# Cutting the first store of an RMSNorm-GELU kernel in three and joining the last two

## Chip, cores and metric

The kernel runs on one core of a Trainium2 chip. The metric is device time in microseconds (us), the median of several executions. "The packet records" below are the single DMA packets that the trace of the profiled execution holds, each with queue, start, duration and size.

## The reference

```python
rms = np.sqrt(np.mean(x ** 2, axis=-1, keepdims=True) + eps)
out = gamma * x / rms
return 0.5 * out * (1 + np.tanh(np.sqrt(2 / np.pi) * (out + 0.044715 * out ** 3)))
```

`x` is 8 x 1024 x 2048 in float32: 67.1 MB are read and 67.1 MB are written, with little arithmetic on each element.

## The kernel before

The 8192 rows are cut into 16 groups of 512 rows, four rows (32 KB) on each of 128 partitions, 4 MB a group. Six slots of SBUF hold groups in flight; slots lie two by two in one tile, so that two groups can share a transfer. SyncE issues the loads, ScalarE (ACT) the stores. ScalarE and VectorE (DVE) square and sum, VectorE multiplies by gamma, ScalarE applies the GELU in place, and the slot is stored.

```python
LOAD_PAIR = 1
STORE_PAIR = 6
NARROW = 128
    ...
def gelu(g):
    for r in range(R):                  # R = 4 rows
        nc.scalar.activation(out=slot[g % SLOTS][:, r, :], in_=slot[g % SLOTS][:, r, :],
                             func=ACT.Gelu_apprx_tanh, scale=rstd[:, g, r : r + 1])

def store(g):
    if g:
        if g // 2 != STORE_PAIR:
            nc.scalar.dma_start(out=part(o2, g), in_=slot[g % SLOTS])
        elif g % 2:
            nc.scalar.dma_start(out=pair_part(o2, g // 2), in_=pair[g // 2 % (SLOTS // 2)])
        return
    src = pair[0].rearrange("p r d -> p (r d)")
    dst = part(o2, 0).rearrange("p r d -> p (r d)")
    for a, z in ((0, NARROW), (NARROW, R * D)):
        nc.scalar.dma_start(out=dst[:, a:z], in_=src[:, a:z])
    ...
for g in range(G + 1):                  # G = 16
    ...                                 # squares, 1/rms and gamma of group g
    if g:
        gelu(g - 1)
        store(g - 1)
        if g - 1 + SLOTS < G:
            load(g - 1 + SLOTS)
```

Group 0 leaves in two stores, the first with 512 bytes of each partition. Groups 12 and 13 leave in one store. The load of group 6 needs slot 0, so it waits for all of group 0's stores.

## Time and profile before

| | before |
|---|---|
| time, median of the first 3 executions | 317.21 us (316.85 to 317.45) |
| span of the profiled execution | 315.1 us |
| busiest compute engine | ScalarE, 66% |
| DMA queues, share of 16 engines' time | loads 49.7%, stores 49.3% |
| bytes moved | 134.24 MB |

The two queues' shares add up to 99.0% of the time of the core's 16 DMA engines; the prediction works out what follows.

### The profile page before, as it was taken

What the parts mean: (1) busy time and instruction counts of PE and PEld (TensorE: products, weight loads), DVE (VectorE), ACT (ScalarE), POOL (GpSimd) and SP (SyncE); (2) the same over time, 40 slices, a digit from 0 to 9 for tenths busy, and PEclk for the clock granted to TensorE, in tenths of its full rate; (3) what the DMA queues carried; (4) which work ended last, traced back from release to release, by engine and by line L of the source; (5) the groups of instructions that cost most, each with busy time, mean ns of one, the idle gap of its engine ahead of it and who ended that gap; (6) DMA issues with size and microseconds to landing.
All of it is one profiled execution on the core that took longest, in us unless ns stands there. A gap on an engine that the chain in (4) does not pass through costs nothing.

```text
span 315.1 us, 457 instructions
## 1 busy us (share of the span) xinstructions
PE 7.2 (2%) x8; PEld 2.5 (1%) x8; DVE 198.5 (63%) x129; ACT 206.9 (66%) x150; POOL 16.4 (5%) x21
## 2 busy tenths in 40 slices
PE   0900000000000000000000000000000000000000
PEld 0300000000000000000000000000000000000000
DVE  0089887988989884639684393668727638781000
ACT  1327869999999749397590965929369295797000
POOL 0010101011010101010010100101001010010000
DMA  8999989999999999999999999999999999999896
GB/s 334 404 462 408 526 339 396 458 402 462 403 463 403 459 408 458 412 453 424 441 424 441 424 441 424 441 428 437 437 428 437 428 437 428 474 399 474 387 445 291
DMA packets 4498, 134.24 MB, mean 426 GB/s; under 512 B 512, under 2 KB 656, under 8 KB 656
## 3 DMA queue, kind: packets, MB, share of 16 engines
q1 hardware_dynamic: 2160, 67.11, 49.7%
q10 hardware_dynamic: 2336, 67.12, 49.3%
q14 instruction: 2, 0.02, 0.0%
HBM read 67.12 MB, written 67.11 MB: 426 GB/s over the span
## 4 chain that ended last, share of the span: by engine, by line
another core or an unknown queue 36%; DMA 36%; ACT 18%; issue 1%; SPq 1%; ACTq 0%
DMA pair<-in_x_dram 21%; DMA out_dram<-pair 15%; ACT pair L133 12%; ACT junk L87 6%; SPq L83 1%; ACTq L143 0%
## 5 line engine op out<-in xcount | busy, mean ns | idle before, releaser
L124 DVE TENSOR_TENSOR pair<-pair,gamma_ps 128x8192 f32<-128x8192 f32 (+1 forms) x19 | 139.2, 7334 | 0.0
L87 ACT ACTIVATE junk<-pair 128x2048 f32<-128x2048 f32 x42 | 79.0, 1881 | 78.7 <-DMA pair<-in_x_dram 76.2
L133 ACT ACTIVATE pair<-pair,rstd 128x2048 f32<-128x2048 f32 x64 | 122.6, 1987 | 2.3 <-DVE pair L124 1.9
L97 DVE SCALAR_TENSOR_TENSOR spare<-pair 128x2048 f32<-128x2048 f32 x22 | 50.4, 2291 | 39.3 <-DMA pair<-in_x_dram 24.6
L110 POOL TENSOR_TENSOR y<-ms,power 128x4 f32<-128x4 f32 x16 | 16.1, 1007 | 260.8 <-DVE ms L105 260.8
L105 DVE TENSOR_SCALAR ms<-ssq 128x4 f32<-128x4 f32 x16 | 2.7, 170 | 26.2 <-ACT junk L87 25.4
L113 DVE TENSOR_TENSOR z<-ms,y 128x4 f32<-128x4 f32 x16 | 2.6, 163 | 19.0 <-POOL y L110 19.0
L87 ACT ACTIVATION_READ_ACCUMULATOR junk<-pair 128x1 f32 x42 | 7.8, 186 | 0.0
L171 PE MATMUL gamma_ps<-spare,ones 1*128 1x512 f32 x8 | 7.2, 1072 | 8.3 <-DMA spare<-in_gamma_dram 8.3
L117 DVE SCALAR_TENSOR_TENSOR rstd<-z,y 128x4 f32<-128x4 f32 x16 | 2.6, 162 | 0.6
L114 DVE SCALAR_TENSOR_TENSOR z<-z,y 128x4 f32<-128x4 f32 x16 | 2.6, 162 | 0.6
L171 PEld LDWEIGHTS gamma_ps<-spare,ones 1*128 1x128 f32 x8 | 2.5, 326 | 11.4 <-issue 11.4
L169 ACT ACT_TABLE_LOAD x1 | 1.3, 1283 | 1.4 <-PEq L211 1.4
L97 DVE DVE_READ_ACCUMULATOR spare<-pair 128x1 f32 x22 | 1.8, 83 | 0.0
L167 DVE MEMSET warm<- 1x1 f32 x1 | 0.1, 59 | 0.8 <-PEq L211 0.8
L169 ACT ACTIVATE warm<-warm 1x1 f32<-1x1 f32 x1 | 0.2, 202 | 0.0
L168 DVE MEMSET ones<- 1x128 f32 x1 | 0.2, 165 | 0.0
L166 POOL MEMSET power<- 128x4 f32 x1 | 0.1, 101 | 0.3 <-POOLq L211 0.3
L211 POOL MEMSET const-float32-0.0<- 128x1 f32 x1 | 0.1, 98 | 0.2 <-issue 0.2
L211 POOL MEMSET const-bfloat16-1.0<- 128x1 bf16 x1 | 0.1, 102 | 0.0
L211 POOL MEMSET const-uint8-127<- 128x1 uint8 x1 | 0.1, 102 | 0.0
L211 POOL MEMSET const-float32-1.0<- 128x1 f32 x1 | 0.1, 98 | 0.0
## 6 DMA issues: line engine op xcount, KB each, us to landing
pair<-in_x_dram SPq DMA_DIRECT2D x14, 4096.0 KB, 25.5
out_dram<-pair ACTq DMA_DIRECT2D x13, 4096.0 KB, 52.4
out_dram<-pair ACTq DMA_DIRECT2D x1, 4032.0 KB, 31.3
out_dram<-pair ACTq DMA_DIRECT2D x1, 64.0 KB, 17.6
spare<-in_gamma_dram ACTq DMA_DIRECT2D x1, 8.0 KB, 7.4
pair<-in_x_dram SPq DMA_DIRECT2D x1, 40.5
out_dram<-pair ACTq DMA_DIRECT2D x1, 30.9
```

Source lines behind the costliest of these rows:

```text
L83: nc.sync.dma_start(out=slot[g % SLOTS], in_=part(x2, g))
L87: nc.scalar.activation(out=junk, in_=slot[g % SLOTS][:, q, :], func=ACT.Square, accum_out=ssq[:, g, q : q + 1],)
L97: nc.vector.scalar_tensor_tensor(out=spare[:, :, 0:GW], in0=row, scalar=1.0, in1=row, op0=ALU.bypass, op1=ALU.mult, accum_out=ssq[:, g, q ...
L105: v.tensor_scalar(out=ms, in0=ssq[:, g, :], scalar1=1.0 / D, scalar2=eps_f, op0=ALU.mult, op1=ALU.add,)
L110: nc.gpsimd.tensor_tensor(out=y_, in0=m_, in1=power, op=ALU.pow)
L113: v.tensor_tensor(out=z_, in0=m_, in1=y_, op=ALU.mult)
L114: v.scalar_tensor_tensor(out=z_, in0=z_, scalar=-0.5, in1=y_, op0=ALU.mult, op1=ALU.mult)
L117: v.scalar_tensor_tensor(out=rstd[:, g, :], in0=z_, scalar=1.5, in1=y_, op0=ALU.add, op1=ALU.mult,)
L124: nc.vector.tensor_tensor(out=rows, in0=rows, in1=gamma_ps.unsqueeze(1).to_broadcast([P, n, D]), op=ALU.mult,)
L133: nc.scalar.activation(out=slot[g % SLOTS][:, r, :], in_=slot[g % SLOTS][:, r, :], func=ACT.Gelu_apprx_tanh, scale=rstd[:, g, r : r + 1],)
L169: nc.scalar.activation(out=warm, in_=warm, func=ACT.Gelu_apprx_tanh)
L171: nc.tensor.matmul(out=gamma_ps[:, k : k + 512], lhsT=ones, rhs=gamma_row[:, k // GW : (k + 512) // GW, 0:GW], start=True, stop=True,)
```

## The change

The intent: group 0's two first rows can leave before the last two are done; the last two groups save a transfer. The number of transfers stays at 32. (`part` follows because the rows of a joined pair lie together: groups 14 and 15 are now also loaded by the rows of a pair, with the same packet size.)

```diff
-STORE_PAIR = 6
+STORE_PAIRS = (6, 7)
@@ part
-        if g // 2 in (LOAD_PAIR, STORE_PAIR):
+        if g // 2 in (LOAD_PAIR, *STORE_PAIRS):
@@ store
-            if g // 2 != STORE_PAIR:
+            if g // 2 not in STORE_PAIRS:
@@
-        for a, z in ((0, NARROW), (NARROW, R * D)):
+        for a, z in ((0, NARROW), (NARROW, R * D // 2), (R * D // 2, R * D)):
```

## The prediction

> **What bounds the kernel now.** I read first the page: the span, the busy shares, the DMA rows of the slices, and the packet counts.
>
> ```profile
> span 315.1 us, 457 instructions
> PE 7.2 (2%) x8; PEld 2.5 (1%) x8; DVE 198.5 (63%) x129; ACT 206.9 (66%) x150; POOL 16.4 (5%) x21
> DMA  8999989999999999999999999999999999999896
> DMA packets 4498, 134.24 MB, mean 426 GB/s; under 512 B 512, under 2 KB 656, under 8 KB 656
> q1 hardware_dynamic: 2160, 67.11, 49.7%
> q10 hardware_dynamic: 2336, 67.12, 49.3%
> ```
>
> No compute engine is above 66%, while the 16 DMA engines are at nine tenths or more nearly everywhere. Loads (q1) and stores (q10) take 99.0% of the DMA engines' time together. Next, the busy-by-stretch view, in the middle of the run (its last two columns are the DMA share and GB/s; a short stretch misleads there, because a packet is counted whole where it starts), then the DMA view of the stretch from the landing of the last load to the landing of the second-last stores:
>
> ```profile
> 90.00:250.00 160.00, 0.00 (x0) 0.00 (x0) 108.35 (x66) 108.55 (x78) 8.44 (x9) 1.00 1.00 433
> ```
>
> ```profile
> DMA packets 240, 11.01 MB, mean 433 GB/s; under 512 B 32, under 2 KB 32, under 8 KB 32
> q10 hardware_dynamic: 240, 11.01, 100.1%
> ```
>
> So 433 GB/s is what the engines give, with both queues working and with the store queue alone. The chain of waits then shows what holds the loop together:
>
> ```profile
> 127.99 0.33 SPq L83
> 128.32 18.86 another core or an unknown queue
> ...
> 147.25 0.33 SPq L83
> 147.58 18.99 another core or an unknown queue
> ```
>
> Loads are issued 19.26 us apart. One load and one store are 8.39 MB, and 8.39 MB / 433 GB/s is 19.37 us: the period is the transfer time, with nothing left over. The waits of the SyncE queue name the releaser, a store that frees a slot:
>
> ```profile
> SPq L83 <- DMA out_dram<-pair: 236.9, 11, 47.3
> ```
>
> The whole: the first packet starts at 1.74 us; 134.24 MB / 433 GB/s is 310.0 us; the last packet ends at 313.9, the last store lands at 314.3, and the closing barrier is 0.8. 313.9 - 1.7 - 310.0 leaves 2.2 us. The trace's packet records show where most of it is: the first packets of the run take 1.5 to 2.2 us instead of 1.21 (about 0.75 us averaged over 16 engines), and from 46 to 49.4 us a round of load packets takes about 1.75 us instead of 1.21 (about 0.65). The latter comes just after the 512-byte store of group 0. The measured 317.21 is the span plus some 2 us outside it.
>
> [...] on one engine I read, from 50.6 us on, a load packet (1213 ns), a store packet (1194), a load packet and so on; and earlier a 512-byte packet (27 ns) after each load packet. [...] The trace shows receipts (a packet's end to the landing, about 0.3 us at the end), but no engine idles for one, as the next transfer is queued. [...]
>
> **The change, part by part.** *Count.* Group 0 goes from two stores to three, groups 14 and 15 from two to one. Each of those transfers has 128 data packets and 16 semaphore packets (14 x 144 + 144 = 2160 on q1), so both queues keep their counts: 2160 and 2336, with the same bytes.
>
> *Packet time.* The records have 27 ns for 512 B, 1194 for 32256 B, 1213 for 32768 B and 2418 for 65536 B: a straight line of 36.8 ps per byte plus 8 ns a packet. An engine has 8 packets of each store. Group 0 now: 8 x (27 + 1194) = 9.77 us per engine. After: 15872 B is 592 ns, 16384 B is 611, so 8 x (27 + 592 + 611) = 9.84. Added: 0.07 us. Groups 14 and 15 now: 16 x 1213 = 19.41; after: 8 x 2418 = 19.34. Removed: 0.07 us. Sum: 0.00.
>
> *Start of group 0's stores.* The narrow store is issued at 32.79 us, as row 0 ends, and the remainder at 38.47, as row 3 ends. The new second store waits for row 1 only, so goes out near 34.7. It gains nothing there: the eight 512-byte packets of an engine each wait for a load packet of up to 2.4 us, so the ring reaches the next store only at 49.4 us on that engine either way. The extra issue is 0.34 us on ACT, which then idles 3.7 us before 42.16.
>
> *Order on the engine.* Round robin is per packet, not per byte. Eight packets of 32256 B against load packets of 32768 B shared the engine half and half, from 49.4 to 67.4. With packets of half the size the loads get two thirds: laying the packets of that engine out by hand, the second store ends at 61.4, the last load packet of group 5 at 67.4 (before 73.4), then the third store runs alone to 71.1. So group 5 should land near 69 instead of 75.3, and group 0's store near 73 instead of 69.7; the load of group 6 goes out some 3.5 us later than its 69.8. No byte is lost: the store queue holds the stores of groups 1 and 2 (issued at 55.8 and 67.9), which fill the load's gap.
>
> *Tail.* Group 14's store was issued at 281.29 and group 15's at 289.38. Merged, it goes out at 289.0 (one issue of 0.34 us less before group 15's rows). The store of groups 12 and 13 lands at 294.95, its first engines done at 293.9. From issue to first packet takes about 1 us at the run's start (0.74 to 1.74), so the merged store is ready at about 290.4, 3.5 us ahead of need. Then 8.39 MB / 433 = 19.37 us gives 314.3, the old landing.
>
> Sum: +0.07 - 0.07, start, dip and barrier unchanged: **317.2 us**, the same.
>
> **The rivals.** *The tail starves.* If the ring had been empty by 281.29, merging would cost the 8.1 us to 289.38: 325 us. Against it is the view of 269.6 to 295 above: 100.1% busy on earlier stores alone. It needs group 15 to finish 3.5 us later than it does. *The later load tears a hole.* If the 3.5 us delay of group 6's load went round the ring of slots to the end: near 321 us. Against it: stores land 48.6 us after issue at the median, so more than two stores lie queued, and steady transfers make good such a shift. *The dip moves.* The slow round of load packets at 46 to 49.4 us sits where the 512-byte packets end. If the size of the next store's packets matters, it can vanish or come twice: 316.6 or 317.9. I take it as unchanged. *A shared semaphore stalls ACT.* Transfers take eight semaphores in turn, and each waits for the earlier user; one more transfer early shifts the turn by one. ACT's chain shows 0.14 us at 73.99 and 0.52 at 284.95 around such waits. A stall of a few us on ACT in the middle hides behind queued stores; at the end it must exceed the 3.5 us. *The intent:* with smaller second packets the loads come earlier, but compute isn't the bound, so an earlier group 5 buys nothing.
>
> **Range and chances.** Everything that moves is a matter of order in queues that stay full; what can alter the sum is the dip (0.65 us either way) and the spread of runs (316.85 to 317.45). So 8 times in 10 from 316.4 to 318.1. Two per cent is 6.3 us: faster by that is impossible with 310.0 us of transfer in it, short of fewer bytes; slower needs the tail to starve nearly in full. Chances: faster 0.005, same 0.98, slower 0.015.
>
> **What would show it.** Right: 4498 packets and the same counts per queue; 433 GB/s in the middle and the tail; issue of the merged store near 289.0, last landing near 314.3; the load of group 6 issued near 73 us; the second store issued near 34.7. Wrong: a zero in the DMA row of any slice but the ends, an issue of the last store after 293, or loads spaced by more than 19.4 us. A difference of over 1 us with a DMA row full of nines would mean that packets take longer by size or order than the line above says.

What the part on order rests on, that packets of the two queues take turns whatever their size, is in the packet records of the kernel before, chained into engines by their times: on one engine, from 36.5 to 46.4 us, each of eight 512-byte packets (27 ns) goes between two load packets (2418 or 1213 ns; once, at 41.41 us, a 4-byte load packet of 9 ns), and from 49.4 to 67.4 us load packets (1213 ns) and store packets (1194 ns) alternate in the same way.

## The result

| | before | after |
|---|---|---|
| median of 6 executions | 317.19 us | 316.89 us |
| lowest to highest | 316.85 to 317.45 | 316.74 to 317.04 |
| last landing of a store, from the span's start | 314.27 us | 314.18 us |

The ratio is 0.9991, with a 95% interval from 0.9978 to 1.0004: the same. Here and below, a ratio is the mean time of one kernel's runs over that of the other's of the same rounds, so not quite the ratio of the medians quoted.

The page of the changed kernel, with the lines that answer to those of the kernel before (the DMA row has one digit for each fortieth of the span):

```profile
span 315.0 us, 458 instructions
DMA  8999989999999999999999999999999999999996
DMA packets 4498, 134.24 MB, mean 426 GB/s; under 512 B 512, under 2 KB 656, under 8 KB 656
q1 hardware_dynamic: 2160, 67.11, 49.7%
q10 hardware_dynamic: 2336, 67.12, 49.4%
```

The busy-by-stretch view of the changed kernel, the same 160 us (the last column is GB/s):

```profile
90.00:250.00 160.00, 0.00 (x0) 0.00 (x0) 108.29 (x66) 108.64 (x78) 8.55 (x9) 1.00 1.00 433
```

Packets, bytes and rate are the same to the digit. The DMA row has an 8 or 9 in every slice but the last. What moved is the order. The timeline of ScalarE in the changed kernel shows the three stores of group 0 (start, duration of the issue, line):

```profile
32.87 0.36 ACTq L152 DMA_DIRECT2D out_dram<-pair  x1
...
34.76 0.34 ACTq L152 DMA_DIRECT2D out_dram<-pair  x1
...
38.54 0.34 ACTq L152 DMA_DIRECT2D out_dram<-pair  x1
```

The second store does leave 3.8 us before the third. The timelines of the last stores, of the kernel before and then of the changed kernel:

```profile
281.29 0.34 ACTq L143 DMA_DIRECT2D out_dram<-pair  x1
...
289.38 0.34 ACTq L143 DMA_DIRECT2D out_dram<-pair  x1
```

```profile
273.46 15.24 ACT L133 ACTIVATE pair<-pair,rstd 128x2048 f32<-128x2048 f32 x8
288.73 0.34 ACTq L145 DMA_DIRECT2D out_dram<-pair  x1
```

Without an issue in between, ScalarE runs the eight rows of groups 14 and 15 in one piece; their store goes out 7.4 us later than the first of the two did before, and its data land at 314.18 us, where group 15's landed at 314.27. Up to its first packet, earlier stores kept the engines busy. For the changed kernel, the line of the DMA view of 269.6 to 295 us that the prediction showed for the kernel before reads (a packet counts whole where it starts, hence over 100%):

```profile
q10 hardware_dynamic: 233, 11.31, 102.8%
```

One thing had not been foreseen. The waits of the SyncE queue in the changed kernel have a new line:

```profile
SPq L83 <- DMA out_dram<-pair: 230.2, 12, 41.2
...
SPq L83 <- DMA spare<-in_gamma_dram: 5.6, 1, 5.6
```

The load of group 5 waited 5.6 us for gamma, with which it has nothing to do: the trace's DMA issues name eight semaphores, used in turn (107 to 110, 100, 102, 105, 106, by the order of the program, from the load of group 8 on in the kernel before), and the extra store of group 0 shifted the turn so that this load shares gamma's (100, where it had 110). It went out at 8.2 us instead of 2.7. Four loads were queued ahead of it, so no DMA engine noticed.

### The profile page after: what moved, and what is told of

It reads as the page before. It is cut to its first block, busy times and chain, and to the rows that moved or that the text cites. A ratio compares the mean times of both kernels' runs of the same rounds, so it can differ in the third digit from the quotient of the medians.

```text
span 315.0 us, 458 instructions
## 1 busy us (share of the span) xinstructions
PE 7.2 (2%) x8; PEld 2.5 (1%) x8; DVE 198.4 (63%) x129; ACT 206.8 (66%) x150; POOL 16.4 (5%) x21
## 2 busy tenths in 40 slices
DMA packets 4498, 134.24 MB, mean 426 GB/s; under 512 B 512, under 2 KB 656, under 8 KB 656
## 3 DMA queue, kind: packets, MB, share of 16 engines
q10 hardware_dynamic: 2336, 67.12, 49.4%
## 4 chain that ended last, share of the span: by engine, by line
another core or an unknown queue 36%; DMA 36%; ACT 18%; SPq 1%; issue 1%; ACTq 0%
DMA pair<-in_x_dram 21%; DMA out_dram<-pair 14%; ACT pair L133 12%; ACT junk L87 6%; SPq L83 1%; ACTq L143 0%
```

## The experiments

The theory: from the first packet to the last, the DMA engines always have a packet queued, so that issuing a store earlier, later, whole or cut only changes the order. The rivals: the tail starves or nearly so; the head gains something; and one of the two hides the other's cost. Then there are two questions the prediction left: what makes the dip at 46 to 49.4 us, and how much slack the merge spent.

| run | transfers | median us | ratio to before | 95% interval |
|---|---|---|---|---|
| after_again | 32 | 316.91 | 0.9992 | 0.9976 to 1.0007 |
| head_only | 33 | 317.13 | 0.9997 | 0.9982 to 1.0011 |
| tail_only | 31 | 317.19 | 0.9999 | 0.9982 to 1.0016 |
| no_narrow | 31 | 317.10 | 1.0002 | 0.9985 to 1.0020 |
| after_late1 | 32 | 316.96 | 0.9998 | 0.9983 to 1.0013 |
| after_late4 | 32 | 319.83 | 1.0089 | 1.0072 to 1.0106 |
| before_late4 | 32 | 316.99 | 1.0006 | 0.9986 to 1.0025 |
| halved | 43 | 327.61 | 1.0324 | 1.0297 to 1.0351 |
| half_parts | 43 | 360.38 | 1.1231 | 1.1166 to 1.1296 |
| halved_three | 35 | 317.29 | 1.0007 | 0.9994 to 1.0019 |
| all_pairs_ordered | 28 | 329.40 | 1.0365 | 1.0329 to 1.0400 |

The first four ran on one chip beside 11 executions of the kernel before (median 317.10), the next three and halved beside 7 (316.86), half_parts beside 7 (317.05), the last two beside 11 (317.14). All results in the table are correct.

### The change again, and its halves

after_again is the changed kernel. head_only takes the tail back, tail_only the head:

```diff
 head_only:  -STORE_PAIRS = (6, 7)
             +STORE_PAIRS = (6,)
 tail_only:  -((0, NARROW), (NARROW, R * D // 2), (R * D // 2, R * D))
             +((0, NARROW), (NARROW, R * D))
```

> The changed kernel once more, beside its own halves on one chip. Main theory (the DMA engines are full from the first packet to the last, only order changes): within 0.3 us of the kernel before, ratio 0.999 to 1.001. Rival (the smaller spread between the engines and the earlier loads are worth something): 0.3 us faster again, ratio 0.999, interval clear of 1.

> Group 0 in three stores, groups 14 and 15 stored apart (33 transfers). Main theory: the packet line adds 0.07 us for the third store and takes nothing away, so 317.2 within 0.3, and stores of group 14 issued near 281 that land where the first half of the merged store would. Rival (the head brings the 0.3 us seen): as fast as the changed kernel. Rival (a stall at a shared semaphore, the turn being shifted by one): a load or store issued late, yet no DMA gap.

> Group 0 in two stores, groups 14 and 15 in one (31 transfers). Main theory: 0.07 us less than before, so 317.1 within 0.3; the merged store goes out near 289 and the last landing is near 314.2. Rival (the tail starves): over 318. Rival (the tail brings the 0.3 us seen): as fast as the changed kernel. The load of group 6 goes out near 69.8 as before, group 5's landing is near 75.

Each half alone is within 0.1 us of the kernel before, where the theory put it; neither starves and neither gains. The pages count 4642 packets for head_only and 4354 for tail_only, 144 more and 144 fewer than 4498, one transfer each way. The 0.07 us that the prediction gave a transfer is below what these intervals resolve. The changed kernel was 0.3 us under the kernel before in its first runs and 0.2 in the repeat, but neither interval is clear of 1 and no half shows it, so it stays unexplained and may be nothing.

### How much slack the merge spent

A number of dummy passes of ScalarE over the slot, just before group 15's rows, make the last store late without changing what is moved:

```diff
     def gelu(g):
+        for _ in range(N if g == G - 1 else 0):     # N = 1 or 4
+            nc.scalar.activation(out=junk, in_=slot[g % SLOTS][:, 0, :], func=ACT.Square)
         for r in range(R):
```

> The changed kernel with one dummy pass (about 1.9 us) on ScalarE before group 15's rows, result unused. Main theory: the merged store goes out near 290.6 instead of 288.7, its first packet could start near 292, the queue empties only at 293.9: no change, 316.9 within 0.3. Rival (the merged store is already on the path): 1.9 us more, 318.8.

> The changed kernel with four dummy passes (about 7.5 us) before group 15's rows. Main theory: issue near 296.2, first packet near 297.4, the queue empty since 293.9, so 3 to 3.5 us more: 320.1, with a gap in the DMA row near 295 us. Rival (already on the path): 7.5 us more, 324.4. Rival (ScalarE still has more slack than read): no change.

> The kernel before with the same four dummy passes. Main theory: group 14's store goes out at 281.3 as ever and keeps the queue full to 303.6, group 15's goes out near 297, so no change: 317.2 within 0.3. Against after_late4 this shows what the merge gave away: slack of one store, 9.7 us, no time. Rival (ScalarE is the bound at the end): 7.5 us more.

ScalarE's timeline in after_late4 and in before_late4, with the issue of the last store:

```profile
296.47 0.34 ACTq L147 DMA_DIRECT2D out_dram<-pair  x1
```

```profile
281.27 0.34 ACTq L145 DMA_DIRECT2D out_dram<-pair  x1
...
297.01 0.34 ACTq L145 DMA_DIRECT2D out_dram<-pair  x1
```

The busy-by-stretch view around it, in the same order (last two columns: DMA share and GB/s):

```profile
290.00:299.00 9.00, 0.00 (x0) 0.00 (x0) 0.00 (x0) 6.44 (x4) 0.00 (x0) 1.00 0.54 233
```

```profile
290.00:299.00 9.00, 0.00 (x0) 0.00 (x0) 0.00 (x0) 6.98 (x4) 0.00 (x0) 1.00 0.92 397
```

In after_late4 the last store is 7.74 us later than in the changed kernel (296.47 against 288.73) and the time 2.94 us longer (319.83 against 316.89), so 4.8 us of lateness were free. The packet records, chained into engines by their times (they carry no engine number), show each engine idle for 2.7 to 3.8 us from about 294 us on, until its first packet of the merged store. With one pass (issue at 290.60) there is no loss. In the kernel before, an issue at 297.01 costs nothing: group 14's store, out at 281.27, covers it. The merge therefore did take slack away, none of which was in use. How much is an estimate, up to 9.7 us (the time of group 14's store, 4.19 MB at 433 GB/s); measured is that 7.6 us of lateness (297.01 against 289.38) are free before the merge and 4.8 after it.

### The dip at 46 us

no_narrow leaves the 512-byte store out, so that group 0 goes in two stores of two rows:

```diff
-        for a, z in ((0, NARROW), (NARROW, R * D // 2), (R * D // 2, R * D)):
+        for a, z in ((0, R * D // 2), (R * D // 2, R * D)):
```

> The changed kernel without the 512-byte store: group 0 in two stores of two rows (31 transfers). It tests where the slow round of load packets at 46 to 49.4 us comes from. If the end of the 512-byte packets makes it: it is gone, and the time is 0.6 us less than the changed kernel's (316.3). If any change from loads alone to loads and stores makes it: it moves to the first store's packets near 36 us and the time stays. If it belongs to the clock time 46 to 49 or to those loads: it stays where it is.

I summed, over the packet records, what each packet took over the usual duration of its size, and divided by 16 engines. The kernel before lost 0.67 us in this way from 46 to 53 us and nothing from 30 to 46; the changed kernel 0.62 and 0.01. no_narrow lost nothing from 46 to 53, and 0.80 from 30 to 46. The busy-by-stretch views show the same, more roughly (GB/s last), of the changed kernel and of no_narrow:

```profile
36.00:44.00 8.00, 0.00 (x0) 0.00 (x0) 8.00 (x2) 4.25 (x3) 0.00 (x0) 1.00 1.04 448
44.00:52.00 8.00, 0.00 (x0) 0.00 (x0) 4.23 (x7) 7.94 (x8) 1.01 (x1) 1.00 1.01 402
```

```profile
36.00:44.00 8.00, 0.00 (x0) 0.00 (x0) 7.46 (x1) 2.35 (x2) 0.00 (x0) 1.00 1.04 406
44.00:52.00 8.00, 0.00 (x0) 0.00 (x0) 2.89 (x7) 7.88 (x8) 1.01 (x1) 1.00 0.96 414
```

So the dip has moved with the first store of large packets; the second of the three theories holds. It is not made by the end of the 512-byte packets, nor by the clock time. The time did not change, as that theory said. The long packets are those of loads, from about 3 us before the first large store packet starts. What the engines do in that round stays open.

### When a cut does cost something

The same kernel with 11 stores cut in two, each half going out when its two rows are done:

```diff
-                nc.scalar.dma_start(out=part(o2, g), in_=slot[g % SLOTS])
+                for h in (0, R // 2):
+                    nc.scalar.dma_start(out=part(o2, g)[:, h : h + R // 2, :],
+                                        in_=slot[g % SLOTS][:, h : h + R // 2, :])
```

> The changed kernel with the stores of groups 1 to 11 each in two of two rows (43 transfers instead of 32). Packet line: 11 times 73 ns, 0.8 us more, 317.7. [...] Rival (a transfer waits for the eighth before it, as they share a semaphore: eight transfers are now 2.7 groups, about 52 us, less than a store's 56 us to landing): ScalarE stalls at these waits and the stores go out later; if the queued stores run out, several us more with gaps in the DMA row, else nothing.

It takes 10.7 us more, so the count of transfers is not free after all. ScalarE's timeline in halved shows the fourth row of a group and the issue of its second half:

```profile
97.96 1.99 ACT L133 ACTIVATE pair<-pair,rstd 128x2048 f32<-128x2048 f32 x1
111.65 0.34 ACTq L144 DMA_DIRECT2D out_dram<-pair  x1
```

The row is done at 99.95 us, and the store goes out 11.7 us later. It waits for the semaphore that it shares with an earlier load, which landed at 111.58 us. This repeats in later groups. The rates in the page of halved:

```profile
GB/s 323 450 434 466 388 392 417 443 420 446 420 415 404 431 440 416 438 402 422 406 424 456 408 428 424 438 446 410 434 404 444 430 412 430 503 404 394 498 289 16
```

The end shows the larger part of the loss: the last store's first engine landed at 316.5 us, its last at 325.0, and in the packet records 13 of the 16 engines have ended by 317 and the slowest at 324.6. In the changed kernel the landings are 0.9 us apart. The lag is older than the last store: of a transfer that landed around 195 us, the last engine is 5 us behind the second-last, and of one around 221 us, 9.5 us. In the middle the busy-by-stretch view is:

```profile
60.00:300.00 240.00, 0.00 (x0) 0.00 (x0) 159.44 (x104) 170.10 (x122) 13.08 (x13) 1.00 1.01 427
```

That is 427 GB/s, where the changed kernel has 434 in the same stretch, at a DMA share of 1.01, and in the packet records the gaps between an engine's packets add up to 0.6 us at most: the late issues left no DMA engine without work. By the packet records, packets longer than usual cost about 3.5 us per engine more than in the changed kernel, most of it in the few microseconds after the load queue has run dry and starts again (393 GB/s from 94 to 98 us and 378 from 98 to 102, for instance). The 11 extra transfers themselves are 0.9 us of packets, close to the 0.8 expected.

Are the late issues the cause, or the 16384-byte packets? The first attempt to tell, half_parts, kept large packets by cutting the partitions instead of the rows:

```diff
+                for h in (0, P // 2):
+                    nc.scalar.dma_start(out=part(o2, g)[h : h + P // 2],
+                                        in_=slot[g % SLOTS][h : h + P // 2])
```

> As halved, 43 transfers, but each store of groups 1 to 11 is cut by partitions (64 and 64) after all four rows are done: packets keep 32768 bytes, and no store goes out before the whole group is ready. If the waits for the eighth transfer back made halved slow (they put the second half's issue behind a landing, so the store queue runs dry and starts anew): slow again, 320 or more. If the 16384-byte packets made it slow (loads run ahead of the stores on each engine): near 317.

It says nothing on the question, as it brought a cost of its own. Its rates on the page:

```profile
GB/s 344 412 509 361 454 402 408 462 206 397 391 375 387 325 354 401 401 408 383 383 394 383 419 354 401 401 415 408 404 401 390 401 339 314 398 300 448 368 65 29
```

In the ninth slice, most of which such stores have to themselves, the rate is 206 GB/s, about half of 433, at a busy share of 0.88, and their packets take about 2.5 us instead of 1.21: alone, a store from 64 neighbouring partitions got about half the rate here; why, no trace shows. (Beside loads, as in most of the run, the median packet of these stores takes the usual 1.21 us.) How much of the 43 us this explains is not shown; stores wait for shared semaphores here too, up to 23 us. (Its executions spread from 354.29 to 364.83 us. Two of the four, the profiled one among them, lie over 1.5% above the fastest and so count as slow; the ratio in the table uses the other two.)

The second attempt, halved_three, keeps the small packets but spaces them, and was meant to leave no shared semaphore that binds:

```diff
+                n = R // 2 if g in (2, 5, 8) else R
+                for h in range(0, R, n):
+                    nc.scalar.dma_start(out=part(o2, g)[:, h : h + n, :],
+                                        in_=slot[g % SLOTS][:, h : h + n, :])
```

> The changed kernel with only the stores of groups 2, 5 and 8 halved (35 transfers). The eighth transfer back is now at least 3.5 groups, 68 us, behind, more than a store's 56 us to landing. If the waits on shared semaphores made halved slow: nothing to wait for here, so only three times 73 ns: within 0.4 us of the changed kernel. If the 16384-byte packets made it slow: three elevenths of its 10.7 us, 2.9 us more, near 320.

Its median is 0.4 us over the changed kernel's and 0.15 over the kernel before on its chip, and its middle is back at full rate:

```profile
90.00:250.00 160.00, 0.00 (x0) 0.00 (x0) 119.28 (x73) 120.23 (x87) 9.06 (x9) 1.00 1.01 433
```

So a 16384-byte packet as such does not cost 2.9 us per three groups. But the run cannot tell the two suspects apart, because the late issues that it was meant to exclude are there. ScalarE's timeline in halved_three:

```profile
173.80 7.66 ACT L133 ACTIVATE pair<-pair,rstd 128x2048 f32<-128x2048 f32 x4
192.66 0.34 ACTq L145 DMA_DIRECT2D out_dram<-pair  x1
```

The rows are done at 181.46 us, and the store goes out 11.2 us later, behind a load that holds its semaphore until it lands at 192.6. Four more stores go out 2.6 to 3.3 us late. The expectation's "nothing to wait for here" was wrong, and none of these waits cost time. So a late issue like the one of 11.7 us in halved is not enough for a loss either.

What halved_three never has is loads that start again beside small store packets. After 60 us, its load queue pauses six times for 2.5 us or more, that of the changed kernel ten times; each time the store packets around the restart have 32768 bytes, and packets longer than usual cost at most 0.03 us per engine (from 2 us before the first new load packet to 8 us after it). In halved all ten restarts are beside 16384-byte packets and cost 0.00 to 0.95 us, 3.3 us together; the dearest, from 94 us on, comes before the late issue at 111.65, with a single one, of 4.1 us, earlier. That makes small packets beside restarting loads the likelier place of this part of the loss, but no run tests it alone. The cause of the 10.7 us, and why one engine ends 8 us after the others, stay open.

One more thing in the profiled execution of halved_three came from no edit: the eight matmuls that spread gamma took 21.7 us instead of 7.2, for a reason not known, so that group 0's first store went out at 47.44 us instead of 32.87. This cost nothing either (317.35 us), as the theory of full queues has it. And the dip moved along, to 58 to 60.5 us, just before the first large store packet at 61.4.

### More merging, for a faster kernel

If merges save 0.07 us each, pairs from group 4 on should save 0.3 us more. A first build, all_pairs, gave a wrong result: it issued the load into a pair's first slot before the pair was stored. Its time (334.05 us) measures nothing.

> The changed kernel with groups 4 to 15 in pairs (28 transfers). Packet line: four merges of 8 x 8 + 9 ns less, 0.3 us, so 316.6, if the queues stay full. Rival (a slot comes free only when both groups of its pair have landed, and the first group's store starts 19 us later, so the stores queued run out and loads bunch): gaps in the DMA row and several us more, over 319.

all_pairs_ordered issues both loads after the pair's store:

```diff
-STORE_PAIRS = (6, 7)
+STORE_PAIRS = (2, 3, 4, 5, 6, 7)
@@ main loop
-                if g - 1 + SLOTS < G:
-                    load(g - 1 + SLOTS)
+                k = g - 1
+                late = k // 2 in STORE_PAIRS
+                for j in (() if late and k % 2 == 0 else (k - 1, k) if late else (k,)):
+                    if j + SLOTS < G:
+                        load(j + SLOTS)
```

> all_pairs built rightly: the loads into a pair's two slots go out only after the pair's store has been issued (all_pairs overwrote the first group's slot before its store). Packet line: 0.3 us less than the changed kernel, 316.6, if the queues stay full. A first sum of a pair's round: 39 us loading beside stores, about 20 us computing its second group, 39 us storing beside loads, 98 us against 116 us for three pairs, so some slack is left. Rival (loads and stores bunch, the queues run dry by turns, as the DMA row of all_pairs already shows from the middle on): holes in the DMA row, over 325.

It is slower, at 329.40 us. ScalarE's timeline gives the issue of the store of groups 12 and 13, and the busy-by-stretch view the 13 us before:

```profile
287.25 0.34 ACTq L145 DMA_DIRECT2D out_dram<-pair  x1
```

```profile
274.00:287.00 13.00, 0.00 (x0) 0.00 (x0) 7.88 (x7) 12.94 (x10) 1.01 (x1) 1.00 0.06 28
```

The DMA engines stand nearly idle for 13 us (28 GB/s): all earlier stores have landed by 271.1 us, and the last loads, bunched at the end, land at 273.5 and 283.2, so nothing is ready to be stored. This is the starving that the prediction named as a rival. It is real, but one pair merged at the end is 4.8 us away from it, while merging in the middle holds back the loads and runs into it. No kernel tried beats the changed one.

## Why the prediction was right, point by point

- **The bound.** Right: 433 GB/s in the middle, packets and bytes unchanged, a DMA row without a hole. Of the runs that lost 2 us or more, after_late4 and all_pairs_ordered left the DMA engines without work, half_parts moved stores at about half rate (206 GB/s) where they ran alone, and halved lost its time with full queues, to longer packets and to one engine that fell behind. Full queues are therefore not by themselves a guarantee of 433 GB/s.
- **The packet sums, +0.07 and -0.07.** Consistent: the counts moved by 144 packets as said, the durations for 15872 and 16384 bytes were 592 and 611 ns as interpolated, and both halves stay within 0.1 us of before. The size itself is not resolved.
- **Earlier start of group 0's second store.** Right: issued at 34.76 us (said 34.7), first packet at 49.38 on the engine that was read (said 49.4), no gain.
- **Order on the engine.** Right in kind: on that engine group 5's last load packet ended at 67.4 and the third store at 71.06, as laid out; group 5 landed at 68.7 (said 69). The term that was mis-sized is "the load of group 6 goes out some 3.5 us later": it was 2.0 us (71.83 against 69.80). The next load went out 1.7 us earlier than before (87.60 against 89.27), so the delay did not go round the slots. The prediction had carried over the 2 us between the first and last engine of group 0's store; it was 0.4 us (landings from 71.34 to 71.75).
- **Tail.** Right: issue at 288.73 us (said 289.0), last landing at 314.18 (said 314.3). The slack was said to be 3.5 us and measured as 4.8. The issue was 0.3 us earlier than said, the first packet followed an issue by 0.9 us rather than 1.4, and the sum had taken the first engine to run out.
- **The losses.** The first load packets of the kernel before lost 0.68 us per engine by the records, not 0.75, so of the 2.2 us beside the transfer time about 0.9 are not accounted for. In the changed kernel the same packets lost 0.51, in its repeat 0.73, so part of the loss varies from run to run.
- **A transfer more or less.** One more (head_only) or one fewer (tail_only) changed less than 0.1 us, and neither interval reaches 1 us either way. Right that no engine idles between transfers: in the packet records of the kernel before, the engines are without a packet for 0.03 us each from 3 to 292 us.
- **The dip.** Taken as unchanged, and it was (0.67 to 0.62 us). Its description as coming "just after the 512-byte store" held as a place, but not as a cause; it comes with the first large store packets.
- **A shared semaphore.** The prediction looked for a stall on ScalarE. It came on SyncE, 5.6 us on the load of group 5, and was hidden behind four queued loads. Waits of ScalarE came in halved (11.7 us) and halved_three (11.2 us); the second was hidden, and that the first was not is not shown.

## What to carry to other kernels

When the DMA engines are full from end to end, sum bytes over the measured rate first (134.24 MB / 433 GB/s, 310.0 us here): no order of transfers tried here got below that (fastest execution 316.70 us). Then treat a store that is issued earlier or later as a change of slack, not of time, and measure the slack with a deliberate delay, since a merge that costs nothing today may leave little for the next one. Measure a cut before relying on it, even where the sum of its packets is small: eleven stores cut along rows cost 10.7 us for a reason that is still open, three cost nothing, and eleven cut along partitions cost 43.
